# Two attention layers on one TensorE: the output matmuls of a chunk of keys are held until both heads' transposed weights are there, and are issued as one run

## The chip, the cores and the metric

The kernel runs on one core of a Trainium2 chip. The metric is the device time of one execution in microseconds, as a median over runs. The core has five engines that work from queues of their own: TensorE (PE in the profile, its weight loads PEld), VectorE (DVE), ScalarE (ACT), GpSimd (POOL) and SyncE (SP), which here issues the DMAs.

## The reference

One sequence of 2048 tokens and 1024 features goes through three parts, all in float32:

- a short convolution mixer: `x = x + (b * conv3(c * xin) * silu(g)) @ w_out_a`;
- a stick-breaking attention of 8 heads of 64, in blocks of 128 queries: with `z = q k^T / 8`, the weight of key j is `sigmoid(z_j)` times the product of `1 - sigmoid(z_m)` over the later keys m that the query sees, and the output is `weights @ v`, gated and projected by `w_out_b`;
- a second block: a pooling mixer beside a sparse attention, in which an indexer scores all earlier keys for each query, the best 256 are kept, and 8 query heads over 2 key heads do a softmax attention on these; then the projection by `w_out`.

```python
weights = jnp.exp(jnp.where(mask, z + rev, -jnp.inf))                 # stick-breaking
outs.append(jnp.einsum("bhqk,bhkd->bhqd", weights, vf[:, :, :kl]))
...
p = jax.nn.softmax(s, axis=-1)                                        # sparse
o = jnp.einsum('bqhgk,bqkhd->bqhgd', p, v_sel.astype(jnp.float32))
```

## The kernel before, in words

The kernel is written as Python generators that emit instructions step by step (`phase_a` to `phase_g`); `merge` takes their steps in turns, so that the instructions of several phases stand mixed in the program. A planner then orders them: each instruction has a priority number, which is its place in the program as it was written, and waits for what it reads; the planner issues on each engine, by its own model of time, the instruction with the lowest number among those that are ready. `high_priority(offset)` sets the counter back by the offset for what is written inside and restores it at the end. `ahead(gen, offset)` wraps every step of a generator in it: with 2000 for the stick-breaking attention, with 0 for the sparse one in its last part. The resulting order is fixed: an engine runs its instructions in that order, and one that waits holds up those behind it.

Both attentions work on 128 queries at a time, on pairs of heads, and on chunks of up to 512 keys (`nb` blocks of 128, 1 to 4). For one chunk, in `phase_c` (first attention) and `f_block` (second):

1. per head, two float32r matmuls give the scores in a PSUM bank `z`; VectorE and ScalarE make the weights from them (sigmoids, a scan along the keys and a product in `phase_c`; mask, maximum and `Exp` over the whole row in `f_block`);
2. per head, TensorE transposes the weights block by block into a bank `tp` (L540, L1151), and ScalarE copies the bank into a buffer of the ring `wt` or `fwt` (L542, L1153), which has three;
3. for each block j and each head a, a float32 matmul adds `v^T weights` to the bank `o` (L546, L1157): 64 output rows per head, head 0 on the upper half of the bank's partitions and head 1 on the lower half.

The matmuls of step 3 are written after both copies, but each waits only for its own head's copy and for the matmul before it on the same bank. In the trace each of these float32 matmuls and transposes shows as the engine's own instructions: a matmul of step 3 as two, a transpose as one. A chunk of 4 blocks so has 16 instructions of step 3, of 3 blocks 12, of 2 blocks 8, of 1 block 4. There are 160 chunks for each attention (40 query-block chunks for each of four pairs of heads).

Beside the attentions, projections of other phases fill TensorE (L118 to L120, three float32r passes). In the second attention, `f_search` finds the threshold of the 256 best scores by counting; the counting instructions write into a ring `junk` of two parts that nobody reads, and the handling of ties (L1016 to L1019) uses two tiles of its own, `tie` and `rank`.

Of the kernel before, what the change touches and what calls it, by code (L numbers as in the profile page):

```python
# [58 lines left out]
def until(gen, stop):  # L59
    """The generator's steps up to the moment when stop() holds; the rest stays in it."""  # L60
# [7 lines left out]
class Build:  # L68
# [14 lines left out]
    def load_w(self, name, nk, c0, m=P, gain=None, after=None, keep=True, own=None):  # L83
        """One column block of a weight matrix, split into two float32r parts; kept in DRAM for the next time."""
# [26 lines left out]
    def lin(self, w, x, nk, c0, n=CH):  # L111
        """PSUM tile of (weight block)^T @ x[:, c0:c0+n] in three float32r passes."""
# [10 lines left out]
    def sums(self, tiles):  # L123
        """Sums of squares per token, tokens on partitions: of [P, HT] tiles over rows and tiles; [P, 8] in PSUM."""
# [8 lines left out]
    def rstd(self, tiles):  # L133
        """[P, 8] 1/rms, tokens on partitions."""
# [6 lines left out]
    def bcast(self, r, name, chunk=None):  # L141
        """[P tokens, 8] -> [P, HT]: the value of each token on every partition; or for one chunk [P, CH]."""
# [30 lines left out]
    def turn(self, name, n):  # L173
        """The next of n parts of a tile that is there all the time."""
        i = self.turns[name] = (self.turns.get(name, -1) + 1) % n
        return self.rings[name][:, i]

    def psum(self, use):
        """A PSUM bank for a use: products, scores, transposed blocks or attention outputs."""
        return self.ps.tile([P, CH], F32, name=use, tag=use, bufs=BANKS[use])  # L180

    def bank(self):
        """A PSUM bank; where only products need banks, from all of them by turns."""
# [4 lines left out]
    def part(self, *shape):  # L188
        """A part of the tile of what is there all the time."""
# [6 lines left out]
    def setup(self):  # L196
# [22 lines left out]
        # heads of the rows in blocks of queries and of keys  # L219
# [55 lines left out]
    def adaln(self):  # L275
        """mod = silu(c) @ w_ada + b_ada, features on partitions."""
# [25 lines left out]
    def add_square(self, acc, x, k, scale=1.0):  # L302
        """Adds the squares of block k to the tile in the list acc, which block 0 begins."""
# [8 lines left out]
    def norm_x(self, src, rb, dst):  # L312
        """dst = split of src * rb; src is the [D, HT] source in DRAM."""
# [14 lines left out]
    def phase_a(self, h, pool_x, pool_y):  # L328
# [19 lines left out]
        for c in range(NKB):  # L348
# [7 lines left out]
            if c == 0:  # L356
                # 1 / rms of each token goes onto the products
# [54 lines left out]
    def to_tokens(self, src, dst):  # L412
        """[P features, CH tokens] -> rows of dst [CH, P] in DRAM."""
# [50 lines left out]

    def load_dup(self, tag, bufs, src, a, sl):
        """Rows of head a of a pair on both halves of the partitions: [P, high and low part, tokens]."""
# [5 lines left out]
    def load_stack(self, tag, bufs, src, sl):  # L472
        """High parts of each head of a pair above its low parts: [P, head, tokens]."""
# [5 lines left out]
    def c_rings(self):  # L479
        """What the stick-breaking attention takes turns in."""  # L480
# [10 lines left out]
    def phase_c(self, h):  # L491
# [3 lines left out]
        for p in range(4):  # L495
            for g in (2 * h, 2 * h + 1):
# [14 lines left out]
                for i in range(4):  # L511
                    qs = slice(i * P, (i + 1) * P)
                    prev = [None, None]
                    for c in range(g, -1, -1):
# [3 lines left out]
                        for a in range(2):  # L518
# [23 lines left out]
                            nc.scalar.copy(wt[:, :W], tp[:, :W])  # L542
                            wts.append(wt)
                        for j in range(nb):
                            for a in range(2):
                                nc.tensor.matmul(  # L546
                                    o[a * 64 : (a + 1) * 64, qs],
                                    vt[c][:, j, a * 64 : (a + 1) * 64],
                                    wts[a][:, j * P : (j + 1) * P],
                                    start=(c == g and j == 0),  # L550
                                    stop=(c == 0 and j == nb - 1),
                                )
# [11 lines left out]
    def phase_d(self, h, pool):  # L564
# [21 lines left out]
        # v1: mean squares + eps; r1 * r2 with r2 = 1 / sqrt(ss2 * r1^2 / D + eps) is 1 / sqrt(ss2 / D + eps * v1)  # L586
# [22 lines left out]
    def rope(self, xe, half, dst):  # L609
        """Rotates xe, first halves of the heads in its first rows and second halves in as many more; dst: in DRAM."""  # L610
# [17 lines left out]
    def rope_pair(self, x, y, dst):  # L628
        """Rotates the first halves (x) and second halves (y) of four heads; dst: [32, halves, heads, parts, HT] in DRAM."""
# [15 lines left out]
    def head_ms(self, ps, ind, before=None):  # L645
        """Mean squares per head of a block's rows, tokens on partitions: (sum of x^2) / 64 + eps, or + before."""
# [13 lines left out]
    def heads(self, t, g):  # L660
        """Four heads of queries in DRAM: [32, halves, heads, parts, HT]."""
        return t[:, 4 * g : 4 * g + 4].rearrange("(t d) a s n -> d t a s n", t=2)

    def phase_e(self, h):
# [13 lines left out]
        # key and weights of the indexer  # L678
# [16 lines left out]
        # key  # L695
# [17 lines left out]
        # value  # L713
# [708 lines left out]
```

## Time and profile before

| | |
|---|---|
| time, three runs | 3493.83, 3502.8, 3504.3 us (median 3502.8) |
| the profiled execution, its span | 3500.3 us |
| TensorE busy | 3318.3 us, 95% of the span |
| TensorE weight loads busy | 2594.3 us, 74% |
| VectorE busy | 2258.6 us, 65% |
| ScalarE busy | 1485.0 us, 42% |
| GpSimd busy | 488.3 us, 14% |

The page gives the span from the first to the last instruction of one profiled execution; which of the three timed runs stands beside it is not told, and the median lies 2.5 us above the span. Busy time of TensorE counts an instruction from its start to the end of its way through the array, so that neighbours overlap: sixteen instructions of step 3 in a row take 1.09 us together though one alone is shown with about 0.27 us. The spacing of the starts is what one costs.

### The profile page before, as it was taken

What the parts mean: (1) busy time and instruction counts of PE and PEld (TensorE: products, weight loads), DVE (VectorE), ACT (ScalarE), POOL (GpSimd) and SP (SyncE); (2) the same over time, 40 slices, a digit from 0 to 9 for tenths busy, and PEclk for the clock granted to TensorE, in tenths of its full rate; (3) what the DMA queues carried; (4) which work ended last, traced back from release to release, by engine and by line L of the source; (5) the groups of instructions that cost most, each with busy time, mean ns of one, the idle gap of its engine ahead of it and who ended that gap; (6) DMA issues with size and microseconds to landing.
All of it is one profiled execution on the core that took longest, in us unless ns stands there. A gap on an engine that the chain in (4) does not pass through costs nothing.

```text
span 3500.3 us, 49153 instructions
## 1 busy us (share of the span) xinstructions
PE 3318.3 (95%) x17922; PEld 2594.3 (74%) x17922; DVE 2258.6 (65%) x4508; ACT 1485.0 (42%) x2668; POOL 488.3 (14%) x600
## 2 busy tenths in 40 slices
PE   8999999999999999989998999888899999989997
PEld 7888888888787777766776777666777777667675
DVE  5444544553536887789876777887636868798641
ACT  4111421111313444556544554563354555765451
POOL 0000110000100000042201111420100421112002
PEclk9999999999999999998999999899999999999998
DMA  3111442343464544555444534753433553114005
GB/s 107 49 49 58 155 152 85 126 129 112 153 175 129 160 130 142 160 178 148 124 134 133 182 124 136 220 142 112 163 126 103 181 154 97 45 58 159 25 28 173
DMA packets 369233, 438.68 MB, mean 125 GB/s; under 512 B 23504, under 2 KB 269776, under 8 KB 368976
## 3 DMA queue, kind: packets, MB, share of 16 engines
q1 hardware_dynamic: 368976, 435.38, 40.4%
q8 instruction: 146, 2.39, 0.3%
q14 instruction: 111, 0.91, 0.1%
HBM read 308.94 MB, written 124.78 MB: 124 GB/s over the span
## 4 chain that ended last, share of the span: by engine, by line
PE 76%; DVE 9%; DMA 8%; issue 3%; ACT 2%; POOL 1%; SPq 0%; ACTq 0%; DVEq 0%; POOLq 0%
PE lin L118 9%; PE lin L119 9%; PE lin L120 9%; PE o L1157 4%; PE o L546 4%; PE z L118 4%; PE z L119 4%; PE z L120 4%; PE tp L540 3%; PE tp L1151 3%; PE tp L118 3%; PE tp L119 3%; PE tp L120 3%; PE z L1128 2%; PE z L520 2%
## 5 line engine op out<-in xcount | busy, mean ns | idle before, releaser
L118 PE MATMUL lin<-act,fixedr 128*128 128x512 f32 x1488 | 601.4, 405 | 31.5 <-DMA fixedr<-kept_w_in 15.2
L119 PE MATMUL lin<-act,fixedr 128*128 128x512 f32 x1488 | 600.1, 403 | 2.2 <-DVE act L602 1.8
L120 PE MATMUL lin<-act,fixedr 128*128 128x512 f32 x1488 | 596.9, 401 | 0.0
L103 ACT ACTIVATE fixedr<-fixed 128x512 fp32r<-128x512 f32 x295 | 186.7, 633 | 748.2 <-PE lin L119 277.8
L533 DVE TENSOR_TENSOR_SCAN crf<-crf 128x512 f32<-128x512 f32 (+3 forms) x320 | 358.1, 1125 | 89.8 <-ACT crf L530 87.2
L118 PEld LDWEIGHTS lin<-act,fixedr 128*128 128x128 f32 x1488 | 284.7, 191 | 103.2 <-issue 9.4
L104 DVE TENSOR_TENSOR fixedr<-fixed,fixedr 128x512 fp32r<-128x512 f32 x295 | 202.2, 686 | 207.5 <-ACT fixedr L103 203.1
L119 PEld LDWEIGHTS lin<-act,fixedr 128*128 128x128 f32 x1488 | 284.8, 191 | 67.9 <-DVE act L602 3.5
L120 PEld LDWEIGHTS lin<-act,fixedr 128*128 128x128 f32 x1488 | 284.9, 191 | 64.1 <-issue 1.4
L1130 DVE CUSTOM_DVE_ANT_0 fe<-z,masks 128x512 f32<-128x512 f32 (+3 forms) x320 | 188.2, 607 | 140.7 <-PE z L1129 112.5
L542 ACT COPY crf<-tp 128x512 f32<-128x512 f32 (+3 forms) x320 | 165.7, 530 | 187.4 <-PE tp L540 169.2
L118 PE MATMUL z<-act,fixedr 128*128 128x512 f32 x584 | 230.9, 396 | 11.4 <-ACT fixedr L103 11.4
L1153 ACT COPY ff<-tp 128x512 f32<-128x512 f32 (+3 forms) x320 | 161.5, 522 | 177.0 <-PE tp L1151 100.4
L523 ACT ACTIVATE crf<-z 128x512 f32<-128x512 f32 (+3 forms) x320 | 174.1, 547 | 132.1 <-PE tp L540 101.3
L546 PE MATMUL o<-crf 128*64 128x128 f32 x2176 | 214.2, 287 | 16.7 <-DMA crf<-vst 10.0
L119 PE MATMUL z<-act,fixedr 128*128 128x512 f32 x584 | 229.6, 394 | 0.0
L120 PE MATMUL z<-act,fixedr 128*128 128x512 f32 x584 | 229.6, 393 | 0.0
L1157 PE MATMUL o<-ff,keys 128*64 128x128 f32 x2176 | 222.2, 285 | 5.1 <-ACT ff L1153 5.1
L536 POOL TENSOR_TENSOR crf<-crf 128x1 f32<-128x1 f32 x192 | 85.8, 448 | 1003.7 <-ACT crf L523 863.7
L863 DVE SCALAR_TENSOR_TENSOR sc<-ff,fixed,sc 128x512 f32<-128x512 f32 (+3 forms) x266 | 183.1, 707 | 62.2 <-ACT ff L856 59.9
L856 ACT ACTIVATE ff<-z 128x512 f32<-128x512 f32 (+3 forms) x304 | 158.1, 543 | 129.7 <-PE z L854 115.5
L534 DVE TENSOR_TENSOR crf<-crf 128x511 f32<-128x511 f32 (+3 forms) x320 | 204.9, 646 | 11.2 <-DVE crf L525 0.3
(343 smaller groups left out, 6613.7 us busy)
## 6 DMA issues: line engine op xcount, KB each, us to landing
fixed<-in_w_in_a_dram SPq DMA_DIRECT2D x128, 256.0 KB
fixedr<-kept_w_out SPq DMA_DIRECT2D x64, 512.0 KB
kept_w_in<-fixedr SPq DMA_DIRECT2D x46, 512.0 KB
fixedr<-kept_w_in SPq DMA_DIRECT2D x46, 512.0 KB
crr<-kst SPq DMA_DIRECT2D x80, 256.0 KB
crr<-qst SPq DMA_DIRECT2D x64, 256.0 KB
fixed<-x2d SPq DMA_DIRECT2D x64, 256.0 KB
ffr<-q2s SPq DMA_DIRECT2D x128, 128.0 KB
```

The source lines that it names most:

```text
L103: nc.scalar.activation(t[:, 0], raw, AF.Copy)
L104: nc.vector.tensor_tensor(t[:, 1], raw, t[:, 0].bitcast(F32), ALU.subtract)
L118: self.nc.tensor.matmul(ps[:, :n], whi[k], a, start=k == 0, stop=False)
L119: self.nc.tensor.matmul(ps[:, :n], whi[k], b, start=False, stop=False)
L120: self.nc.tensor.matmul(ps[:, :n], wlo[k], a, start=False, stop=k == nk - 1)
L523: nc.scalar.activation(s[:, :W], z[:, :W], AF.Sigmoid)
L533: nc.vector.tensor_tensor_scan(er, er, er, left, ALU.mult, ALU.min)
L534: nc.vector.tensor_tensor(s[:, : W - 1], s[:, : W - 1], e[:, 1:W], ALU.mult)
L546: nc.tensor.matmul(o[a * 64 : (a + 1) * 64, qs], vt[c][:, j, a * 64 : (a + 1) * 64], wts[a][:, j * P : (j + 1) * P], start=(c == g and j = ...
L863: nc.vector.scalar_tensor_tensor(sc[:, c0 : c0 + m], r[:, :m], w, sc[:, c0 : c0 + m], ALU.mult, ALU.add)
L1130: nc.vector.tensor_tensor_reduce(row[:, c0 : c0 + m], z[:, :m], mb[:, c0 : c0 + m], 1.0, NEG, ALU.subtract, ALU.max, mx[:, c : c + 1])
L1157: nc.tensor.matmul(o[a * 64 : (a + 1) * 64, p * P : (p + 1) * P], self.v2t[c // 2][:, 4 * (c % 2) + j, kv * 64 : (kv + 1) * 64], wts[a][:, ...
```

## The change

It adds a helper `burst`. The last ScalarE copy of a chunk (that of head 1) is remembered, and the first matmul of step 3 gets a dependency on it; the other matmuls follow through their order on the bank. Inside the helper the priority counter is set back by 0 and restored at its end, so that what is written next has the same numbers as the run. It is applied in both attentions.

Beside it, the tiles `tie` and `rank` go, and their data is put into the two parts of the `junk` ring, which become twice as large (4096 bytes per partition each). Comments and docstrings are removed, which has no effect on the program.

```diff
+    @contextlib.contextmanager
+    def burst(self, ready):
+        dep = mybir.DependencyInfo(mybir.DependencyClass.Sync, mybir.DependencyReason.DATA)
+        start = []
+        def first(mm):
+            if not start:
+                self.tc.add_manual_dep(mm.ins, ready.ins.name, dep, reason="burst")
+                start.append(mm)
+        with self.tc.high_priority(offset=0):
+            yield first
...
@@ phase_c
-                            nc.scalar.copy(wt[:, :W], tp[:, :W])
+                            last = nc.scalar.copy(wt[:, :W], tp[:, :W])
                             wts.append(wt)
-                        for j in range(nb):
-                            for a in range(2):
-                                nc.tensor.matmul(
...
+                        with self.burst(last) as first:
+                            for j in range(nb):
+                                for a in range(2):
+                                    first(
+                                        nc.tensor.matmul(
...
@@ junk, ties
-        return self.turn("junk", 2).bitcast(dt)[:, :n]
+        return self.turn("junk", 2).rearrange("p a n -> p (a n)").bitcast(dt)[:, :n]
-        return (self.at.tile([P, S], I16, name=m, tag=m, bufs=1)[:, :n] for m in ("tie", "rank"))
+        t = self.rings["junk"]
+        return (t[:, i].rearrange("p a n -> p (a n)").bitcast(I16)[:, :n] for i in range(2))
...
@@ f_block
-                    nc.scalar.copy(wt[:, : nb * P], tp[:, : nb * P])
+                    last = nc.scalar.copy(wt[:, : nb * P], tp[:, : nb * P])
                     wts.append(wt)
-                for j in range(nb):
-                    for a in range(2):
-                        nc.tensor.matmul(
...
+                with self.burst(last) as first:
+                    for j in range(nb):
+                        for a in range(2):
+                            first(
+                                nc.tensor.matmul(
...
@@ phase_f
-        m = self.at.tile([P, 4 + 2, S], U8, name="masks", tag="masks", bufs=1)
-        self.rings["mask"], self.rings["junk"] = m[:, :4], m[:, 4:]
+        m = self.at.tile([P, 4 + 4, S], U8, name="masks", tag="masks", bufs=1)
+        self.rings["mask"], self.rings["junk"] = m[:, :4], m[:, 4:].rearrange("p (b a) n -> p b a n", a=2)
...
-            g.tensor_copy(m.bitcast(F32)[:, :, 0:1], mark.to_broadcast([P, 4 + 2, 1]))
+            g.tensor_copy(m.bitcast(F32)[:, :, 0:1], mark.to_broadcast([P, 4 + 4, 1]))
```

## Rows read from the trace of the kernel before

**Rows 1.** The page: busy time by engine, and the chain that ended last.

```profile
PE 3318.3 (95%) x17922; PEld 2594.3 (74%) x17922; DVE 2258.6 (65%) x4508; ACT 1485.0 (42%) x2668; POOL 488.3 (14%) x600
...
PE 76%; DVE 9%; DMA 8%; issue 3%; ACT 2%; POOL 1%; SPq 0%; ACTq 0%; DVEq 0%; POOLq 0%
```

**Rows 2.** Windows over the two attentions: length, busy us (instructions) by engine, clock, DMA.

```profile
core 0: us, PE busy (x) PEld busy (x) DVE busy (x) ACT busy (x) POOL busy (x), PEclk, DMA share, GB/s
1100.00:2185.00 1085.00, 1040.86 (x6260) 793.33 (x6259) 850.51 (x1272) 548.63 (x1087) 171.98 (x271) 0.97 0.48 145
2210.00:3436.00 1226.00, 1127.55 (x6621) 860.97 (x6619) 881.78 (x2484) 656.02 (x1146) 239.90 (x230) 0.95 0.36 111
```

**Rows 3.** Windows of 200 us inside the attentions, four of twelve.

```profile
1600.00:1800.00 200.00, 185.02 (x1130) 137.69 (x1126) 165.16 (x233) 107.59 (x212) 33.42 (x61) 0.96 0.47 137
...
2200.00:2400.00 200.00, 178.73 (x916) 140.25 (x915) 176.46 (x539) 110.03 (x241) 66.03 (x57) 0.91 0.56 164
...
3000.00:3200.00 200.00, 176.93 (x1085) 133.37 (x1086) 174.74 (x483) 130.00 (x218) 54.62 (x43) 0.94 0.32 101
3200.00:3400.00 200.00, 191.47 (x1387) 138.38 (x1385) 123.28 (x384) 112.09 (x166) 5.20 (x6) 0.98 0.11 33
```

**Rows 4.** Timeline of TensorE, first attention: start us, us, engine, line, operation, count.

```profile
1561.62 1.09 PE L546 MATMUL o<-crf 128*64 128x128 f32 x14
1562.64 1.10 PE L540 MATMUL tp<-fixed,crf 128*128 128x128 f32 x8
1563.67 0.43 PE L546 MATMUL o<-crf 128*64 128x128 f32 x2
1564.04 0.50 PE L520 MATMUL z<-crr 128*128 128x512 f32 x1
1564.37 0.39 PE L521 MATMUL z<-crr 128*128 128x512 f32 x1
...
1567.42 0.60 PE L540 MATMUL tp<-fixed,crf 128*128 128x128 f32 x4
1567.78 0.48 PE L520 MATMUL z<-crr 128*128 128x512 f32 x1
1568.09 0.40 PE L521 MATMUL z<-crr 128*128 128x512 f32 x1
1568.42 1.09 PE L546 MATMUL o<-crf 128*64 128x128 f32 x16
```

**Rows 5.** Timeline of TensorE, second attention.

```profile
3426.39 0.66 PE L1151 MATMUL tp<-fixed,fe 128*128 128x128 f32 x4
3426.97 0.43 PE L1157 MATMUL o<-ff,keys 128*64 128x128 f32 x2
3427.34 0.66 PE L1151 MATMUL tp<-fixed,fe 128*128 128x128 f32 x4
```

**Rows 6.** Timeline of TensorE: first and last runs of two, by line.

```profile
1112.28 0.43 PE L546 MATMUL o<-crf 128*64 128x128 f32 x2
...
2159.40 0.33 PE L540 MATMUL tp<-fixed,crf 128*128 128x128 f32 x1
2159.66 0.43 PE L546 MATMUL o<-crf 128*64 128x128 f32 x2
...
2213.81 0.43 PE L1157 MATMUL o<-ff,keys 128*64 128x128 f32 x2
...
3429.53 0.43 PE L1157 MATMUL o<-ff,keys 128*64 128x128 f32 x2
```

**Rows 7.** Groups by line: count, busy us, mean ns, idle before and releasers.

```profile
L546 PE MATMUL o<-crf 128*64 128x128 f32 x2176 | 214.2, 287 | 16.7 <-DMA crf<-vst 10.0 <-ACT crf L542 6.7
L1157 PE MATMUL o<-ff,keys 128*64 128x128 f32 x2176 | 222.2, 285 | 5.1 <-ACT ff L1153 5.1
```

**Rows 8.** A stalled run on the timeline of TensorE, then the windows view behind it.

```profile
1575.21 1.97 PE L546 MATMUL o<-crf 128*64 128x128 f32 x14 [4.19 <-ACT crf L542]
...
1575.00:1588.00 13.00, 12.79 (x64) 10.51 (x65) 12.65 (x11) 6.45 (x13) 7.96 (x6) 0.50 0.73 195
```

**Rows 9.** Groups by line: the longest operation on the tiles `tie` and `rank`.

```profile
L1017 DVE TENSOR_TENSOR_SCAN rank<-tie 128x384 int16<-128x384 int16 (+13 forms) x14 | 37.6, 2687 | 0.0
```

More of the change, by code (lines that the diff above doesn't have):

```diff
@@ L1 @@
+import contextlib
 import math
@@ L541, in phase_c @@
                             wt = self.turn("wt", 3)
-                            nc.scalar.copy(wt[:, :W], tp[:, :W])
+                            last = nc.scalar.copy(wt[:, :W], tp[:, :W])
                             wts.append(wt)
-                        for j in range(nb):
-                            for a in range(2):
-                                nc.tensor.matmul(
[L547 to L552, printed above, removed]
+                        with self.burst(last) as first:
[3 more added lines that the diff above has]
+                                        nc.tensor.matmul(
+                                            o[a * 64 : (a + 1) * 64, qs],
+                                            vt[c][:, j, a * 64 : (a + 1) * 64],
+                                            wts[a][:, j * P : (j + 1) * P],
+                                            start=(c == g and j == 0),
+                                            stop=(c == 0 and j == nb - 1),
+                                        )
+                                    )
                         yield 0.65 * nb
@@ L1152, in f_block @@
                     wt = self.turn("fwt", 3)
-                    nc.scalar.copy(wt[:, : nb * P], tp[:, : nb * P])
+                    last = nc.scalar.copy(wt[:, : nb * P], tp[:, : nb * P])
                     wts.append(wt)
-                for j in range(nb):
-                    for a in range(2):
-                        nc.tensor.matmul(
-                            o[a * 64 : (a + 1) * 64, p * P : (p + 1) * P],
-                            self.v2t[c // 2][:, 4 * (c % 2) + j, kv * 64 : (kv + 1) * 64],
-                            wts[a][:, j * P : (j + 1) * P],
-                            start=(c == 0 and j == 0),
-                            stop=(c == nch - 1 and j == nb - 1),
-                        )
+                with self.burst(last) as first:
[3 more added lines that the diff above has]
+                                nc.tensor.matmul(
+                                    o[a * 64 : (a + 1) * 64, p * P : (p + 1) * P],
+                                    self.v2t[c // 2][:, 4 * (c % 2) + j, kv * 64 : (kv + 1) * 64],
+                                    wts[a][:, j * P : (j + 1) * P],
+                                    start=(c == 0 and j == 0),
+                                    stop=(c == nch - 1 and j == nb - 1),
+                                )
+                            )
                 yield 0.44 * nb
```

## The prediction, made before the run

> **What bounds the kernel.** I read the page first, then the windows, then the timeline of TensorE line by line. The page [rows 1] has TensorE busy for 95% of the span and on 76% of the chain that ended last; VectorE has 9% of that chain and DMA 8%. Busy time alone does not say that the work is useful, so the reader should look at the two stretches that the change touches [rows 2]: in the first attention TensorE is busy 1040.9 of 1085 us (96%) with VectorE at 78%, in the second 1127.6 of 1226 us (92%) with VectorE at 72%. TensorE sets the pace, but not everywhere: in 1600 to 1800, 2200 to 2400 and 3000 to 3200 us [rows 3] VectorE is at 83%, 88% and 87% beside 93%, 89% and 88% of TensorE, while in 3200 to 3400 us TensorE has 96% and VectorE 62%.
>
> The Trainium skill ("Trainium Kernel Development and Optimization", Performance Expectations) speaks against this reading: matmul busy time is a poor measure there, and the busy share of weight loads is to be taken. That share is 74% [rows 1], which by the rule leaves a quarter of the engine free. The timeline decides: it shows what fills the rest.
>
> **What a run of two costs.** In the timeline the matmuls of step 3 come in pieces: a run of 2, then something else, then a run of 14 [rows 4]. The run of 2 is the first matmul of head 0, issued as soon as its own copy is done; the other 14 wait for head 1's copy. The reader is to compare lengths. A run of 14 takes 1.09 us and a run of 16 takes 1.09 us [rows 4]: within a run the two heads' instructions overlap so well that the first matmul is free inside it. By itself it is dear, and I read the price off twice.
>
> - Between transposes and a score matmul [rows 4]: from the first of eight transposes (1562.64) to the second `z` matmul (1564.37) with the run of 2 between them are 1.73 us. Without one, four transposes to the second `z` take 0.67 us (1567.42 to 1568.09); four more transposes are 0.44 (1.10 for eight against 0.66 for four behind a run [rows 4, 5]); transposes that come behind a run pay 0.06 (0.66 against 0.60). That is 1.17 us, so the run of 2 costs 0.56.
> - Between transposes and transposes [rows 5]: 0.95 us from four transposes to the next four, where 0.50 (0.44 and 0.06) would do, and 0.06 more on the second four: 0.51.
>
> As I read it, the turn from one kind of matmul to the other and back is what costs: 64 columns wide against 128. I take 0.53 us for each piece.
>
> **The change part by part.**
>
> *The wait.* It makes one run of each chunk. The timeline has 298 pieces of L546 (141 of them of two instructions, from the one at 1112.28 to the one at 2159.66) and 323 of L1157 (181 of two, 2213.81 to 3429.53) [rows 6]: 621 pieces for 320 chunks, so 301 could go. But about 55 of them are not first matmuls: they are cut out of the middle of a chunk, as at 2159.66, where single transposes of another chunk stand between runs of two [rows 6]. The new wait does not forbid that, and the counter that is set back by 0 gives what follows the same priority as the run, so these may stay. Upper bound 301 x 0.53 = 160 us, lower 246 x 0.53 = 130 us; I take the middle, 145, since some of those pieces are there only because the planner was already waiting for the second copy.
>
> *What is queued behind the wait.* The run of 14 already waited for the same copy, so the wait that ends the chunk is not new; TensorE idled only 6.7 us in all for L542 and 5.1 us for L1153 [rows 7]. What is new is that the first matmul is not there to fill the gap. Behind the run stand transposes and scores of the next chunk. The ring of three copies is no tighter: buffer 0 was held until the last matmul of head 0 before, too. ScalarE, VectorE and SP get no instruction more or less, and no DMA moves in the program. The wait is carried by an instruction that waits for ScalarE anyway, so I cost it at nothing.
>
> *The smaller tiles.* Ties now share the junk ring, so ScalarE's next count into junk must wait until VectorE is done with the ties. Nothing below zero is in it (no instruction gets shorter). Above, the longest of the four operations is 14 scans with 37.6 us together [rows 9], if all of it were waited for and TensorE with it. In the written order the counts of the next group come after those ties on VectorE anyway, so I take 0 and keep 10 us for the range. One small GpSimd copy writes 8 instead of 6 elements, once: nothing.
>
> *What does not come through.* 145 us less on TensorE, on 2311 us of both attentions, helps where TensorE is the limit. Three of the twelve windows are as full on VectorE as on TensorE [rows 3]; a quarter of the gain, 36 us, falls there and I count half, so 18 are lost. In the rest TensorE still idles for DMAs and copies that do not get shorter, and a faster TensorE meets them sooner: I take off 15% of 109, 16 us. So 145 - 18 - 16 = 111 us. That 18 and 16 are my choice; the bounds are 0 lost (160) and all lost.
>
> **The sum.** 3500.3 - 111 = 3389 us for the span. The median of the three runs stands 2.5 us above the profiled span, which I add: 3392 us.
>
> **The rivals.**
>
> 1. *Half of it is absorbed.* VectorE becomes the limit over most of the first attention, or the planner, whose whole order shifts, breaks many runs up again. For it: around 1575 to 1588 us VectorE is at 12.65 of 13 us [rows 8]. Against: 78% and 72% over the whole stretches [rows 2]. Half of 145 less the 16 gives about 55 us: 3448.
> 2. *TensorE was not the limit.* Then each freed half microsecond becomes a wait for VectorE or a DMA and the time stays at 3503. This is also what the skill's rule on busy time would make of it. Against: 76% of the chain is TensorE [rows 1]. The same time comes if the planner undoes the runs altogether.
> 3. *The other side: the holes let the clock fall.* With the first matmul held back, TensorE has less to do while a copy runs. One run did wait, 4.19 us for L542, and behind it the granted clock was 0.50 (1.2 GHz) from 1575 to 1588 us, where a run of 14 took 1.97 instead of 1.09 us [rows 8]. Such an event costs 4.2 and half of 13, about 11 us. From 11 events on the 111 us are gone; 15 would give 3392 + 165 = 3557. For it: the copies are made by an engine that also serves other phases. Against: only 11.8 us of such waits now, though 14 of 16 instructions already hang on the same copy [rows 7].
>
> The Trainium skill ("TensorE: Matmul & The Clock Gate", Loop structure matters more than you think) has it as a rule that a wait between matmuls makes TensorE go cold. The window behind the stall agrees with it (0.50) [rows 8]; whether the change makes more such waits, no row shows.
>
> **Chances.** 0.3% of this time, some 10 us, is about what a measurement can tell from no change. The main case (80 to 155 us gained, 3348 to 3423) gets 0.55; half absorbed (3423 to 3492) 0.25; no change 0.08; slower, by the clock or by an order of the planner that does as much harm, 0.12. So faster 0.80, same 0.08, slower 0.12. The likeliest case's own range is 3348 to 3423. The range for 8 in 10 goes from 3345 (all 160 us) to 3495: it leaves out the two last cases and next to nothing below.
>
> **What the profile after would show.** Right: about 320 to 375 pieces of L546 and L1157 and hardly a run of 2; busy time of these two groups down from 436 us [rows 7] to some 310 to 330; transposes of both heads in rows of eight; TensorE below 3200 us busy, VectorE's share up to about 67%. Wrong: runs of two left in number; idle time before these groups far above 22 us; more stretches at half clock; or fewer TensorE microseconds with the same span, which would mean that VectorE or a DMA ends last.

## The result, and the profile after

The changed kernel takes 3472.74 us (median of 4 runs, 3468.80 to 3479.31) beside 3503.45 us (4 runs) of the kernel before on the same chip: a ratio of 0.9923 with a 95% interval of 0.9900 to 0.9945. That is faster by 31 us (0.8%), with the whole interval below 1; the forecast was 111 us. The direction and the range hold, the size does not.

The page of the profile, busy time by engine (span 3472.6 us):

```profile
PE 3222.2 (93%) x17922; PEld 2569.6 (74%) x17922; DVE 2256.2 (65%) x4508; ACT 1482.4 (43%) x2668; POOL 484.3 (14%) x600
```

TensorE has 96 us less to do than in [rows 1] and the span is only 28 us shorter. The share of weight loads is still 74%: that number did not move with a change that took 3% off TensorE. The two groups of step 3, by line:

```profile
L1178 PE MATMUL o<-ff,keys 128*64 128x128 f32 x2176 | 175.6, 288 | 17.7 <-ACT ff L1172 15.0 <-DVE fixed L972 1.9
...
L563 PE MATMUL o<-crf 128*64 128x128 f32 x2176 | 167.1, 284 | 7.1 <-DMA crf<-vst 4.7 <-ACT crf L557 2.3
```

436 us in [rows 7] have become 343. In the second attention the run now waits 15.0 us for ScalarE's copy, where it waited 5.1. TensorE's timeline at the place of [rows 4]:

```profile
1562.48 0.40 PE L119 MATMUL lin<-act,fixedr 128*128 128x512 f32 x1
1562.81 1.09 PE L563 MATMUL o<-crf 128*64 128x128 f32 x16
1563.84 0.50 PE L120 MATMUL lin<-act,fixedr 128*128 128x512 f32 x1
...
1568.87 0.40 PE L119 MATMUL lin<-act,fixedr 128*128 128x512 f32 x1
1572.49 0.66 PE L555 MATMUL tp<-fixed,crf 128*128 128x128 f32 x4 [3.23 <-DVE crf L549]
```

At this place the run of 16 costs what the run of 14 did (1.09 us), the run of 2 is gone, and six microseconds later TensorE has run out of work and waits 3.23 us for VectorE. The windows over the two attentions (length, busy us and instructions by engine, granted clock, DMA share, GB/s), as in [rows 2]:

```profile
1100.00:2155.00 1055.00, 992.03 (x6274) 779.57 (x6272) 850.23 (x1272) 546.31 (x1085) 178.87 (x271) 0.97 0.50 151
2181.00:3407.00 1226.00, 1077.51 (x6597) 847.50 (x6595) 877.47 (x2484) 655.76 (x1148) 225.79 (x227) 0.93 0.34 110
```

The first attention got 30 us shorter. The second is as long as before (1226 us) although TensorE is busy 50 us less in it, and its mean clock fell from 0.95 to 0.93.

**Where the time went.** For the table I split the time from 1104 us on into the two attentions, each up to its last matmul of step 3, and each length into three parts: *work* is TensorE's busy time with a microsecond at half clock counted as half; *idle* is what is not busy; *clock* is the other half of the busy time at half clock. All are worked out from the trace's records of instructions and of the granted clock; pieces are counted in the order of TensorE's instructions (by this count the kernel before has 618, against 621 in the prediction). Each row is one profiled execution, which lies up to 6 us from the median beside it (e7: 3508.21 beside 3502.11).

| kernel | time, us (ratio) | pieces, 1st + 2nd | 1st: length = work + idle + clock | 2nd: length = work + idle + clock |
|---|---|---|---|---|
| before | 3503 | 296 + 322 | 1076 = 1010.9 + 41.8 + 23.5 | 1253 = 1115.5 + 101.8 + 35.7 |
| after | 3472.7 (0.9923) | 188 + 205 | 1047 = 961.5 + 61.0 + 24.5 | 1252 = 1048.2 + 149.7 + 53.7 |
| e15, old runs, other place for ties | 3492.5 (0.9971) | 296 + 322 | 1074 = 1010.4 + 45.0 + 18.6 | 1246 = 1115.2 + 94.2 + 36.4 |
| e1, runs, other place for ties | 3446.5 (0.9832) | 188 + 208 | 1044 = 962.4 + 62.0 + 19.4 | 1230 = 1049.7 + 120.7 + 59.7 |
| e3, e1 with runs in the 1st alone | 3469.5 (0.9904) | 188 + 316 | 1047 = 962.8 + 62.2 + 22.2 | 1250 = 1105.7 + 104.3 + 40.3 |
| e4, e1 with runs in the 2nd alone | 3469.7 (0.9896) | 296 + 215 | 1081 = 1010.2 + 43.0 + 27.6 | 1213 = 1059.4 + 115.6 + 37.6 |
| e12, e1 with 4096 bytes less room | 3469.6 (0.9917) | 188 + 205 | 1050 = 964.3 + 66.1 + 20.1 | 1245 = 1049.6 + 145.8 + 49.3 |
| e6, e1 with whole runs | 3433.8 (0.9806) | 165 + 160 | 1052 = 954.0 + 66.2 + 31.6 | 1207 = 1030.4 + 131.0 + 45.6 |
| e7, before, light 1st | 3502.1 (1.0004) | 289 + 312 | 1063 = 1004.5 + 39.2 + 19.2 | 1269 = 1113.6 + 106.4 + 49.1 |
| e8, e1, light 1st | 3419.3 (0.9765) | 189 + 207 | 1029 = 961.1 + 48.0 + 19.8 | 1217 = 1052.6 + 121.5 + 43.4 |
| e13, before, light 2nd | 3478.3 (0.9944) | 296 + 314 | 1072 = 1012.3 + 43.3 + 16.5 | 1229 = 1111.0 + 85.9 + 31.8 |
| e14, e1, light 2nd | 3396.9 (0.9705) | 188 + 220 | 1045 = 962.2 + 58.5 + 24.0 | 1175 = 1054.1 + 88.1 + 32.7 |

From before to after, work falls by 49.4 and 67.3, together 117 us for 225 pieces: 0.52 us each, as priced. Idle time takes 67 of these back and half clock 19. 48 of the 67 are in the second attention, and 27.5 us of these are one hole. The waits of TensorE in the changed kernel, the longest sums (us in total, times, longest):

```profile
PE lin L119 <- ACT pp L81: 27.5, 1, 27.5
PE tp L1170 <- ACT fe L1161: 21.1, 12, 5.3
PE lin L119 <- DMA fixedr<-kept_w_out: 18.9, 8, 6.9
PE z L535 <- DMA crr<-qst: 16.0, 4, 13.9
PE o L1178 <- ACT ff L1172: 15.0, 12, 3.1
```

Summed over this view in the two attentions, waits for VectorE went from 20.7 to 59.8 us, for ScalarE from 42.8 to 77.1 (the hole is among these), for DMAs from 74.4 down to 66.5. The prediction had looked for the growth at DMAs, at copies and in the windows that are full on VectorE; at the DMAs it did not come.

**The hole.** VectorE's timeline of the changed kernel; `ws` (L817, L821) is the pooled sum of a chunk, made in steps that double its width, `pp` the split that goes into TensorE's product:

```profile
2660.32 0.70 DVE L817 TENSOR_TENSOR ws<-u 128x527 f32<-128x527 f32 x1
...
2689.65 2.56 DVE L1036 TENSOR_TENSOR_SCAN masks<-masks 128x1152 int16<-128x1152 int16 x1
2692.30 1.42 DVE L1037 SCALAR_TENSOR_TENSOR masks<-masks,fixed 128x1152 int16<-128x1152 int16 x1
2693.76 1.42 DVE L1038 SCALAR_TENSOR_TENSOR masks<-sc,fixed,masks 128x1152 uint8<-128x1152 f32 x1
...
2695.22 0.70 DVE L817 TENSOR_TENSOR ws<-ws 128x525 f32<-128x525 f32 x1
...
2702.63 0.68 DVE L821 SCALAR_TENSOR_TENSOR ws<-ws,u 128x512 f32<-128x512 f32 x1
```

and TensorE's at the same time:

```profile
2676.09 0.40 PE L872 MATMUL z<-keys,ffr 128*128 128x512 f32 x1
2704.03 0.79 PE L119 MATMUL lin<-pp,fixedr 128*128 128x512 f32 x1 [27.54 <-ACT pp L81]
```

Between the first step of the sum (2660.32) and the second (2695.22) lie 35 us, most of them the search for block 8 and its ties. In e1 the same steps follow each other:

```profile
2658.08 0.70 DVE L817 TENSOR_TENSOR ws<-u 128x527 f32<-128x527 f32 x1
2658.84 0.70 DVE L817 TENSOR_TENSOR ws<-ws 128x525 f32<-128x525 f32 x1
...
2661.09 0.68 DVE L821 SCALAR_TENSOR_TENSOR ws<-ws,u 128x512 f32<-128x512 f32 x1
```

By the addresses in the changed program (no trace shows them) the output of the second step is laid on the bytes that hold the scores of block 8 until its last tie instruction (L1038) has read them; it stands 107 instructions behind the first step on VectorE, in e1 3 behind.

### The profile page after: what moved, and what is told of

Same layout as the page of the kernel before. It is cut to its first block, busy times and chain, and to the rows that moved or that the text cites. A ratio compares the mean times of both kernels' runs of the same rounds, so it can differ in the third digit from the quotient of the medians.

```text
span 3472.6 us, 49120 instructions
## 1 busy us (share of the span) xinstructions
PE 3222.2 (93%) x17922; PEld 2569.6 (74%) x17922; DVE 2256.2 (65%) x4508; ACT 1482.4 (43%) x2668; POOL 484.3 (14%) x600
## 5 line engine op out<-in xcount | busy, mean ns | idle before, releaser
L119 PE MATMUL lin<-act,fixedr 128*128 128x512 f32 x1488 | 603.6, 406 | 23.5 <-DMA fixedr<-kept_w_in 12.1
L119 PE MATMUL z<-act,fixedr 128*128 128x512 f32 x584 | 231.1, 396 | 10.9 <-ACT fixedr L104 10.9
L881 DVE SCALAR_TENSOR_TENSOR sc<-ff,fixed,sc 128x512 f32<-128x512 f32 (+3 forms) x266 | 176.7, 686 | 59.4 <-ACT ff L874 58.5
L1170 PE MATMUL tp<-fixed,fe 128*128 128x128 f32 x1088 | 185.4, 292 | 30.9 <-ACT fe L1161 21.1
L1161 ACT ACTIVATE fe<-fe,fixed 128x128 f32<-128x128 f32 (+15 forms) x128 | 165.7, 1295 | 76.6 <-DVE fixed L1160 75.8
```

The source lines that it names most:

```text
L119: self.nc.tensor.matmul(ps[:, :n], whi[k], a, start=k == 0, stop=False)
L881: nc.vector.scalar_tensor_tensor(sc[:, c0 : c0 + m], r[:, :m], w, sc[:, c0 : c0 + m], ALU.mult, ALU.add)
L1161: nc.scalar.activation(row[:, :W], row[:, :W], AF.Exp, bias=nbs, scale=sc, accum_out=den[:, hd : hd + 1])
L1170: nc.tensor.transpose(tp[:, j * P : (j + 1) * P], pe[a][:, k0 : k0 + P], self.ident)
```

## The experiments

The kernel before, run beside each experiment, had medians of 3499.3 to 3502.1 us. Room on chip matters below. The kernel before holds a constant tile of 4 + 2 parts (masks and junk) and takes `tie` and `rank` for a time; the changed kernel holds 4 + 4 parts, 4096 bytes per partition more, all the time. The runs with the old tiles were not timed, since they want more room than there is; e1, e3, e4 and others put the ties into tiles that are there anyway: one (x) into the ring of raw weights, the other (y) across both parts of the junk ring of the old size. So these kernels share the junk ring too, with one of the two tiles.

### e1: the runs, with the ties elsewhere

```diff
     def junk(self, n, dt=I8):
-        return self.turn("junk", 2).rearrange("p a n -> p (a n)").bitcast(dt)[:, :n]
+        return self.turn("junk", 2).bitcast(dt)[:, :n]
     def ties(self, n):
-        t = self.rings["junk"]
-        return (t[:, i].rearrange("p a n -> p (a n)").bitcast(I16)[:, :n] for i in range(2))
+        x = self.rings["raw"].rearrange("p n k m -> p (n k m)").bitcast(I16)
+        y = self.rings["junk"].rearrange("p a n -> p (a n)").bitcast(I16)
+        return x[:, :n], y[:, :n]
...
-        m = self.at.tile([P, 4 + 4, S], U8, name="masks", tag="masks", bufs=1)
+        m = self.at.tile([P, 4 + 2, S], U8, name="masks", tag="masks", bufs=1)
...
```

> The changed kernel with the data of the ties placed elsewhere (one part in the raw weight buffer, the other in both parts of a junk ring of the old size), which frees 4096 bytes per partition; the runs are as in the changed kernel. It is the control for the next two. If the placing of the ties is of no weight: 3473 us, within 10 us. If what counts is which order the planner happens to find (the holes in the order, theory B): anywhere within some 25 us of it.

3446.51 us, 0.9832 (0.9803 to 0.9861): 26 us faster than the changed kernel with nearly the same pieces (188 + 208 for 188 + 205) and the same work. The hole is not there.

### e2: the ties in the larger junk ring, without the runs

The kernel before with only the blocks `junk, ties` and `phase_f` of the diff.

> The kernel before with only the ties moved into the larger junk ring; no wait is added, all runs of two stay. Theory C (the sharing of junk took the gain back): slower than before by much of the missing 90 us, 3540 to 3590. Theories A (other engines absorb it) and B (holes in the order): 3503 within 15 us, since the order hardly changes.

3533.40 us, 1.0079 (1.0053 to 1.0105): slower by 28 to 33 us, between the two ranges that were named. The longest wait is again that of the `pp` product, 24.9 us. So this part of the change, costed at nothing, costs about 0.8% by itself.

### e3 and e4: the runs in one attention

From e1, one of the two `with self.burst(last)` replaced by a helper that does nothing.

> As the control, but only the first attention waits and issues in one run; the second is as before. The order has 188 pieces in the first attention instead of 296: 108 x 0.53 = 57 us less work on TensorE. Theory A (VectorE and the rest absorb three quarters of whatever TensorE is freed of, wherever it is): about 3503 - 14 = 3489. Theory B (the gain comes through except where the order has holes, and the holes that took it are in the second attention): 3503 - 28 = 3475, as fast as with both.

> As the control, but only the second attention waits and issues in one run: some 118 pieces less, 62 us less work on TensorE. Theory A: about 3503 - 16 = 3487. Theory B: if the hole of 27.5 us before the pooling product and its half clock come back, about 3503; if this order has no such hole, up to 3503 - 50 = 3453. The trace says which: idle time of TensorE against its 159 us in the kernel before.

3469.50 us (0.9904, 0.9878 to 0.9930) and 3469.70 us (0.9896, 0.9871 to 0.9922): about 30 us each, and 53 together in e1. e3 lies below what either theory gave; e4 lies between theory A's 3487 and the 3453 of theory B for an order without a hole, and its longest sums of waits show none. A part of each 30 us is the place of the ties and not the runs (e15, next): against e15 it is 23 us each, of 57 and 56 us less work by the table, 40% by itself. The two add up to e1's 46; the loss is no effect of the two together.

### e15: the place of the ties alone

The kernel before with `ties` as in e1 and nothing else, the base of e1, e3 and e4.

> The kernel before with the ties in the place that e1 gives them (x in the ring of raw weights, y in the junk ring of the old length) and no run and no wait: the base of e1, e3 and e4. Theory, the gain of e1 is all the runs' and the place of the ties is worth nothing by itself: 3492 to 3508. Rival, the room that this frees (no tile for ties and ranks) makes part of e1's 54 us: 3488 or less.

3492.48 us, 0.9971 (0.9956 to 0.9986), within the theory's bounds but not nothing: some 10 us (5 to 15 by the interval) of e1's gain are the place of the ties, and 46 us the runs. Of 113 us of work that e1 saves against e15, 40% come through.

### e5: a wait put into e1

```diff
...
+            if (q, k) == (0, 1) and not self.exact:
+                self.late("gx", i)
...
```

The helper `late`, cut here, makes ScalarE's split wait for block 8's last tie instruction.

> The kernel of e1 (3446.5 us) with one dependency more: the split of the second activation tile of the output projection, on ScalarE, waits for the last mask instruction of block 8 of the selection on VectorE. In the changed kernel the same wait came from the place of that tile: it was laid on the bytes of block 8's scores. Theory, the place of the tile makes the hole and the hole is what the changed kernel has lost against e1: TensorE stands for about 25 us before the product of the pooled chunk (pp), then runs at 1.2 GHz for some 30 us, and the time goes back up by 25 to 30 us to about 3473. Rival, it is the ties that share the junk tile in other ways (counts that wait, scans that start late): the hole is there or not, but the time stays within 8 us of 3446.

3454.31 us, 0.9858 (0.9837 to 0.9879). No hole arose (the longest sums of waits have none like it); the planner knew of the wait and could order around it, so this run says nothing of the hole. With e1's work within 1 us in sum (964.9 and 1047.6) and another order it takes 8 us more at the median; the runs of the two overlap (3440.30 to 3452.66 for e1, 3445.55 to 3460.51), so 8 us bound the effect of the order here and do not measure it.

### e9 and e10: the wrong tile moved

I then held the second activation tile of the output projection (`gx`), whose split on ScalarE also waits there, for the cause, and handed out two of these tiles crosswise, in the changed kernel and in e2.

```diff
+        if q == 0 and not self.exact:
+            hi = [hi[0], hi[6], hi[2], hi[3], hi[4], hi[5], hi[1], hi[7]]
+            lo = [lo[0], lo[6], lo[2], lo[3], lo[4], lo[5], lo[1], lo[7]]
```

> The changed kernel with two tiles of the output projection's first chunk handed out crosswise: the activation tile that is split second now lies on bytes that nothing reads late, and the one that is split seventh lies on the bytes of block 8's scores. The order of every engine's instructions is the one of the changed kernel. Theory, the place of that tile makes the 27.5 us hole: the hole and the half clock behind it are gone and the time falls by 25 to 32 us, to 3441 to 3448. Rival, the ties in the junk tile cost by themselves (ScalarE's counts that wait for VectorE's ties, or the scans): the hole closes, the wait turns up at another place, and the time stays above 3460.

> The kernel of e2 (the kernel before with the ties in the larger junk tile, 3533 us) with the same two tiles crosswise. Theory, the place of the tile is all that e2 lost: back to 3500 to 3508, the kernel before. Rival, the shared junk costs by itself: 3515 or more.

3469.57 us (0.9918) and 3531.52 us (1.0090): both as without the edit, and the hole is there as before (26.9 and 24.9 us). As I read the program, the place on chip goes by the order of use, so that the crosswise tiles changed places too; the edit left the hole where it was and decides nothing. Reading VectorE's own order (above) then showed the tile that matters: that of the pooled sum.

### e12: e1 with 4096 bytes less room

```diff
-        m = self.at.tile([P, 4 + 2, S], U8, name="masks", tag="masks", bufs=1)
-        self.rings["mask"], self.rings["junk"] = m[:, :4], m[:, 4:]
+        m = self.at.tile([P, 4 + 4, S], U8, name="masks", tag="masks", bufs=1)
+        self.rings["mask"], self.rings["junk"] = m[:, :4], m[:, 4:6]
...
```

> The kernel of e1 with a constant tile that is 4096 bytes per partition longer and whose added part nothing uses: the ties stay out of the junk ring, and only the room on chip is as short as in the changed kernel. e9 and e10 moved the wrong tile: the place went with the order of use, and the hole stayed. In the program the second step of a pooled chunk on VectorE now stands 107 instructions behind the first (3 in e1), because its output lies on the bytes of block 8's scores. Theory, the lack of 4096 bytes makes the hole and is the whole of what the changed kernel has lost against e1: a hole of 25 to 28 us before the pp product and 3468 to 3478. Rival, the ties in the junk ring cost by themselves: 3447 to 3455.

3469.58 us, 0.9917 (0.9898 to 0.9936): the changed kernel's time, with the ties placed as in e1. (Not outside the junk ring, as the expectation has it: x is out of it, y still lies across both its parts.) Bytes that nobody uses cost 23 us. The first of TensorE's waits, and VectorE's steps:

```profile
PE lin L119 <- ACT pp L81: 26.4, 1, 26.4
```

```profile
2661.71 0.71 DVE L817 TENSOR_TENSOR ws<-u 128x527 f32<-128x527 f32 x1
...
2695.14 1.42 DVE L1039 SCALAR_TENSOR_TENSOR masks<-sc,fixed 128x1152 uint8<-128x1152 f32 x1
...
2696.60 0.70 DVE L817 TENSOR_TENSOR ws<-ws 128x525 f32<-128x525 f32 x1
```

The second step again comes right behind block 8's last tie instruction. Room makes the hole. Moving x into the junk ring as well costs, if anything, the 3 us between this kernel and the changed one, which these runs cannot tell from nothing; that y lies in the ring is common to e1 and e12 and makes no hole in e1.

### e6 and e11: the counter

e6 sets the counter back by 60 instead of 0; e11 has the wait alone, without the counter.

```diff
-        with self.tc.high_priority(offset=0):
+        with self.tc.high_priority(offset=60):
             yield first
```

> The kernel of e1 with the counter set back by 60 places at the run in place of 0, so that the planner lets nothing cut a run: 325 pieces in the program for 320 chunks, where e1 has 396. At the 0.53 us of the prediction for each piece 71 pieces fewer are 37 us: about 3410 if all comes through. If half is swallowed by waits, as in e1, e3 and e4: about 3428. If the pieces that are left in e1 cost nothing, or what the runs now push aside (score products, transposes) comes too late: 3440 or above, with TensorE's idle time up from the 198 us of e1 by as much as its busy time falls.

> The kernel of e1 with the wait alone, without the counter that is set back at the run. The prediction gave the counter no part in the gain. Theory, the wait does it: 188 pieces in the first attention as in e1, no more than 215 in the second, and within 12 us of the 3447 us of e1 (e5, which has the pieces of e1 and another order, lay 8 us above it). Rival, the counter is needed to keep what follows from cutting in: 250 pieces or more in the second attention, and 15 us or more slower than e1.

e11: 3450.51 us, 0.9860 (0.9844 to 0.9876), 188 and 207 pieces: the wait does it, and the counter at 0 nothing. e6: 3433.78 us, 0.9806 (0.9790 to 0.9823), the fastest kernel here that leaves no work out. 71 pieces fewer than e1 take 28 us of work away, and 13 us come through. The group of the second attention, in e6 and then in e1, shows one of the places where the rest stays:

```profile
L1179 PE MATMUL o<-ff,keys 128*64 128x128 f32 x2176 | 159.0, 286 | 30.3 <-ACT ff L1173 30.1
```

```profile
L1179 PE MATMUL o<-ff,keys 128*64 128x128 f32 x2176 | 178.9, 290 | 17.6 <-ACT ff L1173 17.3
```

20 us less busy than in e1, and 13 us more waiting for the copy.

### e7 and e8: VectorE relieved in the first attention

In both, the product of s and e runs on 127 columns in place of up to 1023; the rest of the product is left out.

```diff
-                            nc.vector.tensor_tensor(s[:, : W - 1], s[:, : W - 1], e[:, 1:W], ALU.mult)
+                            nc.vector.tensor_tensor(s[:, : P - 1], s[:, : P - 1], e[:, 1:P], ALU.mult)
```

> The kernel before with one VectorE product of the first attention (s times e, line 534) done on 127 of up to 1023 columns; the rest of that product is left out. It takes about 140 us of VectorE time out of the first attention and nothing of TensorE's. It is the base for e8. If TensorE sets the pace of the kernel before, the time falls little, to 3470 to 3495, by less than 30 us; if VectorE is as much the limit, by 50 us or more.

> The kernel of e1 with the same product cut to 127 columns (left out as in e7). Theory, VectorE's fullness swallows the missing half of the gain: with VectorE relieved in the first attention, the first attention's part of the gain goes from about 29 us towards the 55 us that its 108 removed pieces are worth, so that e8 lies 70 to 80 us below e7. Rival, what swallows it is DMA, copies and the clock behind holes, not VectorE: e8 lies about 54 us below e7, as e1 below the kernel before.

e7: 3502.11 us, 1.0004 (0.9992 to 1.0017), no fall at all where a small one was expected. e8: 3419.29 us, 0.9765 (0.9745 to 0.9784), 83 us below e7, more than the theory gave. The windows over the first attention, of the kernel before, of e7 and of e8:

```profile
1104.00:2180.00 1076.00, 1034.17 (x6230) 788.10 (x6228) 844.22 (x1260) 544.64 (x1078) 171.98 (x271) 0.97 0.48 145
```

```profile
1104.00:2167.00 1063.00, 1023.79 (x6225) 784.80 (x6224) 745.66 (x1262) 545.68 (x1078) 153.39 (x266) 0.98 0.48 146
```

```profile
1104.00:2133.00 1029.00, 980.96 (x6251) 772.12 (x6251) 744.57 (x1260) 545.38 (x1078) 151.76 (x271) 0.98 0.52 154
```

VectorE lost some 100 us there. The 83 us must not be read as they stand: by the table (86 us between the two profiled spans), 34 are in the first attention (32 from before to e1) and 52 in the second, where no work was taken away and where e7 happens to be 16 us longer than the kernel before. What the pair bears on is TensorE's idle time in the first attention. The relief takes 2.6 us of it from the kernel before (41.8 to 39.2) and 14.0 from e1 (62.0 to 48.0). So idle time grows by 8.8 us from e7 to e8; in the pairs without relief there it grows by 15.2 to 20.2 (before or e15 to e1, e15 to e3, e13 to e14). The sums of TensorE's waits do not put this down to VectorE's load, though: waits for VectorE grow by 12 us from e7 to e8 (5.3 to 17.6) and by 16 from before to e1 (9.9 to 25.9), nearly as much. The larger difference is at the DMAs, whose waits fall by 10 in the light pair (23.3 to 13.2) and grow by 8 otherwise (16.9 to 25.3). So TensorE waits more for VectorE's results also when VectorE has 100 us less to do; what part of the loss its load makes is not shown.

### e13 and e14: VectorE and ScalarE relieved in the second attention

Masked scores and exponentials on 128 of each 512 keys, the rest left out; TensorE keeps all its instructions.

```diff
-                        row[:, c0 : c0 + m], z[:, :m], mb[:, c0 : c0 + m], 1.0, NEG, ALU.subtract, ALU.max, mx[:, c : c + 1]
+                        row[:, c0 : c0 + P], z[:, :P], mb[:, c0 : c0 + P], 1.0, NEG, ALU.subtract, ALU.max, mx[:, c : c + 1]
...
-                nc.scalar.activation(row[:, :W], row[:, :W], AF.Exp, bias=nbs, scale=sc, accum_out=den[:, hd : hd + 1])
+                e = row.rearrange("p (c n) -> p c n", n=CH)[:, :nch, :P]
+                nc.scalar.activation(e, e, AF.Exp, bias=nbs, scale=sc, accum_out=den[:, hd : hd + 1])
...
-                        nc.tensor.transpose(tp[:, j * P : (j + 1) * P], pe[a][:, k0 : k0 + P], self.ident)
+                        nc.tensor.transpose(tp[:, j * P : (j + 1) * P], pe[a][:, c * CH : c * CH + P], self.ident)
```

> The kernel before with less work on VectorE and ScalarE in the second attention: the masked scores (the custom instruction) and the exponential are done on 128 of each 512 keys, and the transposes read those 128 columns again and again (the rest is left out). TensorE's instructions are the same. It is the base for e14. If TensorE sets the pace, 3475 to 3505.

> The kernel of e1 with the same work left out as in e13. Theory, VectorE and ScalarE swallow the missing part in the second attention: with both relieved there, TensorE's idle time in the second attention grows by less than 8 us from e13 to e14 (19 us from the kernel before to e1), and e14 lies 70 to 90 us below e13. Rival, the missing part goes to half clock behind short holes and to transfers: idle time still grows by 15 us or more, and e14 lies 45 to 60 us below e13.

e13: 3478.26 us, 0.9944 (0.9927 to 0.9960). e14: 3396.87 us, 0.9705 (0.9689 to 0.9721), 81 us below e13, as the theory had it. The windows over the second attention, of the kernel before, of e13 and of e14:

```profile
2180.00:3433.00 1253.00, 1151.24 (x6724) 879.24 (x6722) 900.77 (x2527) 675.21 (x1179) 243.65 (x225) 0.96 0.37 115
```

```profile
2176.00:3405.00 1229.00, 1142.85 (x6723) 874.70 (x6722) 811.64 (x2528) 599.05 (x1179) 237.67 (x225) 0.96 0.38 117
```

```profile
2149.00:3324.00 1175.00, 1086.47 (x6697) 851.29 (x6696) 807.03 (x2525) 595.09 (x1176) 240.71 (x226) 0.96 0.38 120
```

Here the work falls by 57 us and the length by 54, with VectorE 90 us and ScalarE 75 us lighter. Idle time grows by 2.2 us; in the four pairs without relief in this attention (before to e1, e15 to e1, e15 to e4, e7 to e8) it grows by 18.9, 26.5, 21.4 and 15.1. Idle time itself, 88.1 us in e14, stands 27 below the lowest of the other kernels with the wait here (e4, 115.6); in e13, 85.9, it stands 8 below the lowest of those with the old runs (e15, 94.2). So most of the growth of idle time goes with the load of these two engines together.

Three things stand against saying more. The length by itself is no evidence: from e7 to e8, where nothing was taken from this attention, 52 of 61 us of work come through here too. Half clock grows by 0.9 us in the light pair, but by 24.0, 23.3, 1.2 and -5.8 in the four others, so that the light pair says nothing of it. And the waits for VectorE grow with the relief as much as without: 6.7 to 29.4 us from e13 to e14, 10.9 to 33.9 from before to e1. What differs is ScalarE: 36.9 to 20.5 in the light pair, 30.0 to 47.4 from before to e1. So the pair speaks for ScalarE more than for VectorE, though e13 waits 7 us more for ScalarE than the kernel before, with less work on it; how the loss divides between the two these runs do not tell.

## Why the prediction was wrong in size

**What a run of two costs: right.** 0.53 us a piece was forecast; the table gives 0.52 (117 us for 225 pieces), and 0.48 for the 293 pieces of e6. The 71 pieces between e1 and e6 were worth 0.39 each (28 us). The two readings by place do not hold so well: 0.46 in the first attention (0.56 was read), 0.58 in the second (0.51). The Trainium skill ("TensorEngine Tiling (Array Packing)", Key Properties) says that a change of the tiling mode drains TensorE; a price for 64 columns between work of 128 that falls away with the piece agrees with it, and no run here tells a drain from another cost of the turn.

**How many go: too many.** 246 to 301 were forecast, 225 went, below the lower bound; 68 runs of two are left of 317. 145 us became 117, a shortfall of 28. The remaining ones are not in the wait's power: the planner, with its priorities as they were, still lets other instructions cut a run. e6, with 325 pieces for 320 chunks, shows that 60 places on the counter remove them.

**The wait: nearly right, not nothing.** It makes the runs by itself (e11). But the copy that ends it is waited for: 15.0 us in the second attention in place of 5.1, and 30.1 in e6.

**The smaller tiles: a step that failed, taken at 0.** The prediction looked for its cost in the sharing of the junk ring, at the scans [rows 9]. The sharing costs nothing that shows (e1 and e15 share the ring with y and have no hole; e12 takes as long as the changed kernel with x elsewhere). What costs is that temporary bytes became constant ones: 4096 bytes less room in the second attention push the pooled sum behind block 8's ties. That is 23 us by e12 against e1, with 26.4 us of TensorE standing in one hole (27.5 in the changed kernel). Against the kernel before it is less, about 16 us, since the place that e1 gives the ties is itself worth 10 (e15); without the runs it is some 30 (e2). The diff had this in plain sight, `4 + 2` to `4 + 4`, and I read the sum of the bytes, which falls, and not when they are held.

**What does not come through: the step that failed most.** 34 us of 145 were taken off, 18 of them for the windows that are full on VectorE [rows 3]. Without the hole the loss is 67 of 113 us (e15 to e1): by the table 43.5 of idle time and 24 of half clock. The sum had no term for half clock, which stood among the rivals alone. Of the waits that it named, those for DMAs fell (74.4 to 66.5 us, before to the changed kernel); those for VectorE (20.7 to 59.8) and ScalarE (42.8 to 77.1, the hole among them) grew, VectorE's in both attentions (9.9 to 24.7 and 10.9 to 34.9) and not in a quarter of the windows. Why they grew is shown in part: making both engines lighter removes most of the growth of idle time in the second attention (e14), but waits for VectorE grow there all the same. That the mean shares of VectorE, 78% and 72% [rows 2], hid too short a lead of TensorE over it is the likely reading, and it is argued, not shown; the cause of the 24 us of half clock stays open too.

Together, by the profiled spans of before, e15, e1 and the changed kernel (3500.3, 3491.1, 3447.3, 3472.6): 31.5 us for the pieces (145 less the 113.5 of work between e15 and e1), 35.7 for what was swallowed beyond the 34 (113.5, less the 43.8 that came through, less 34), and 16.1 for the tiles (25.3 from e1 to the changed kernel, less the 9.2 from before to e15). That is the 83.3 us between the 111 forecast and the 27.7 between the two spans.

**The rivals.** Rival 1, half absorbed (55 us), is what the runs do when they have room: 46 us in e15 to e1. Of its mechanism, VectorE as the limit in the first attention, the runs show only a part: TensorE's waits for VectorE grew there by 16 us, and making VectorE lighter left 12 of that. Rival 2 is refuted: the time fell, TensorE waited only 9.9 us for VectorE in the first attention of the kernel before, and with VectorE 100 us lighter there (e7) that attention got 13 us shorter and the whole time stayed. Rival 3 was half there: the busy time at half clock grew from 139 to 176 us; half of the growth, 18, is lost. No stalls of L563 did that (2.3 us for the copy). The hole is one such place; that short waits made the others is argued from the number of stretches, 31 in place of 22 behind 1100 us. e1 has no hole and as much time at half clock (178 us). Windows of the changed kernel behind the hole:

```profile
2676.00:2704.00 28.00, 0.49 (x3) 0.06 (x1) 26.84 (x62) 4.97 (x9) 2.66 (x3) 0.51 0.03 10
2704.00:2707.00 3.00, 2.97 (x7) 2.39 (x8) 3.00 (x7) 0.00 (x0) 1.02 (x2) 0.50 0.00 0
2707.00:2712.00 5.00, 5.00 (x22) 4.03 (x22) 4.17 (x10) 3.14 (x4) 2.43 (x5) 0.99 0.32 105
```

VectorE is busy for 26.84 of these 28 us, TensorE for 0.49, ScalarE for 4.97: the hole is VectorE's queue. The clock is at its lower level (1.2 GHz) through the hole and for three microseconds behind it.

**The signs that were named.** Pieces 393 (320 to 375 forecast), the two groups 343 us (310 to 330), TensorE 3222 us (below 3200), VectorE's share 65% (67%): all short on the side of less gain. More stretches at half clock, one of the signs for wrong, did come.

What stays open: how the loss divides between VectorE, ScalarE and half clock, and which share of small differences is the planner's order or the spread of single executions. One attention alone moves by as much as 17 us from kernel to kernel with nearly the same work: the second takes 1230 us in e1 and 1213 in e4, 1253 in the kernel before and 1269 in e7.

## What to carry to other kernels

A freed microsecond on the engine that sets the pace need not come through: here 40% did, in stretches where the next engine was at 72 to 78%. To find out why, make that engine lighter in both kernels and compare the pair; but read idle time, half clock and the waits by releaser, and a second pair that leaves the stretch alone, since lengths moved by 17 us with nothing changed there. When a change moves data from temporary tiles into constant ones, compare what is held in each stretch and not the totals, and look in the order of each engine for steps that moved far apart. When instructions belong together, look whether anything still cuts in (e6: 71 pieces and 13 us for one number).

## What the runs showed that I had not expected

- Here the waits for an engine were no measure of its load: with VectorE 100 us lighter in the first attention and 90 us in the second, TensorE's waits for it still grew by 12 and 23 us when the wait was added, against 16 and 23 without the relief.
- 4096 unused bytes per partition cost 23 us (e12). The one difference found that is large enough is the place of one VectorE step in its order: idle time in the second attention grows by 25.1 us from e1 to e12, and the hole is 26.4. The order differs from e1's elsewhere too.
- 19 of the 86 us that the changed kernel gave back were not idle time but work at 1.2 GHz, in 31 stretches behind 1100 us in place of 22.
